# A hybrid decoder block: x's staging tiles moved into v's sum tiles, and the sums of the FFN's down weights moved from the first two dense products to the third and fourth

## The chip, the cores and the metric

The kernel runs on one core of one Trainium2 chip. The metric is the device time of one execution in microseconds (us); the time before the change is the median of three runs. A separate execution under the profiler gave the profile and the trace. Engines are named as in the profile: PE multiplies matrices (PEld loads its weights), DVE, ACT and POOL work on whole tiles, and SP issues nearly all DMA transfers, in one queue, in order.

## What is computed

One decoder block over 1024 tokens of width 1024: a Mamba-2 branch and a gated-linear-attention branch from one input projection, merged with sigmoid gates, then cross-attention to 256 memory tokens, then a SwiGLU feed-forward (FFN) and a last normalisation. Everything is float32. The parts that matter here:

```python
merged = sigmoid(g_ssd) * (y_ssd @ w_up_ssd) + sigmoid(g_gla) * (y_gla @ w_up_gla)
h = x + merged @ w_o                       # after the mixer
q = rmsnorm(h) @ w_xq                      # cross-attention's queries
k, v = split(rmsnorm(mem) @ w_xkv)         # its keys and values
...
h = h + (silu(g) * u) @ w_ffn_out          # D_FF = 2816 rows of w_ffn_out
```

## The kernel before, in words

Data lie transposed: a tile holds 128 features (or two or four times 128) by 512 or 1024 tokens, and `half(j)` is one of two halves of 512 tokens. Float32 products are made of three matmuls: every operand is split into a high and a low part (`split`: ACT writes the high part, DVE or POOL the difference), and high*high, low*high and high*low are summed in PSUM. Many of the large products go by a Strassen-like scheme of seven products of sums of blocks instead of eight (`CHAIN`: B11, B21, T1, B22, T2, T3, T4). Instructions are issued by a tile scheduler, which lists each engine's work in order of estimated time. Engines then run their own lists strictly in order and wait on semaphores. A tile that takes the place of another (same tag, or same slot of a pool) waits until the last reader of the older one is done, also when that reader is a DMA store. `slot("op")`, `slot("aux")` and `slot("m")` hand out large tiles from three pools; `vp` is a pool with tiles by name.

**The start (0 to about 100 us).** Three things run side by side. (1) `kv_unit`: the memory's keys and values, one 1 MB piece of `w_xkv` (`raw`) after another, stored to `vm_d` and `kT_d`. (2) `x_steps`: x is transposed on PE in 16 steps (two halves `j` of the tokens, 8 blocks `k` of features). Each step writes one PSUM bank; DVE makes the normalised block `hb` (profile name `hs`) from it, ACT copies the bank into a staging tile `xs` (L608), and every fourth step SP stores `xs` to `xT_d` (L610, 1 MB). The staging tile comes from `slot("op")`, the pool that also gives the operand tiles B11h, B21h, T1h and so on. (3) `v_steps`: GLA's v product by the chain of seven products; `vq` tiles hold its four output sums (`vq00` to `vq11`), `vsa` a sum of weights. The first product, B11, is copied to `vq10`, the second, B21, to `vq00`. SP's list also holds `late_constants`: two loads of `dcol` from `ssd_D` (L202), 1024 elements of four bytes each, and two small ones.

**The merge (848 to 1209 us).** Four dense products, called dense 0 to 3 here: y_ssd by w_up_ssd, y_gla by w_up_gla, merged by w_o, and the queries by w_xq. Each has 16 steps (8 blocks `o` of output features by two halves of tokens) of 24 matmuls of 128x128x512. Weights come as four `raw` pieces of 1 MB per product and are split into `wd` (two buffers) ahead of use by ACT, then DVE. After each step a `post` takes the PSUM bank (`acc`, four buffers). Dense 0's gates `gs_d` and dense 1's gates `gg_d` are loaded per block `o` into the tile `gates` (two halves, L1253): ACT applies the sigmoid (L1257), DVE multiplies, and dense 0 stores the product to `ysg_d` (L1262). Dense 1 loads it again by `ga` and adds it. Dense 2 adds x (`ga<-xT_d`), stores the sum to `h1_d` (in the order listings `h_d`), and sums squares into `ssum` on POOL, which PE adds up over features in dense 3 (`bank<-ones,ssum`).

**The sums of the down weights (`presum`).** For the FFN's last product the kernel forms four sums of blocks of `w_ffn_out` for each of 11 pieces `k`: load 1 MB into the tile `pre` (L1224), four additions of 128x512, four stores of 256 KB to `down_d` (L1228), and again with the same tile. `waiting(early, 5)` starts it five steps into dense 0; it is run with dense 0, 1, 2 and 3 at one step of `presum` per dense step, and in the trace it ran from 857 to 1029 us, beside dense 0 and 1. `either` picks POOL or DVE for each addition from the planner's costs; all 44 went to POOL.

Of the kernel before, what the change touches and what calls it, by code (L numbers as in the profile page):

```python
# [9 lines left out]
F32 = mybir.dt.float32  # L10
# [6 lines left out]
P = 128  # L17
TOK = 1024
D = 1024
# [59 lines left out]
def block_kernel(ctx: ExitStack, tc: tile.TileContext, t: dict, out: bass.AP):  # L79
# [196 lines left out]
    class Unit:  # L276
# [15 lines left out]
        def a(s, i, j):  # L292
            return s.raw[:, j * s.kh:(j + 1) * s.kh, i * P:(i + 1) * P]
# [145 lines left out]
    def run(main, *rest, prio=0):  # L439

        owed = [0.0] * len(rest)
        for _ in main:
            for i, (g, rate) in enumerate(rest):
                owed[i] += rate
                while owed[i] >= 1.0:
                    owed[i] -= 1.0
                    with tc.high_priority(offset=prio):
                        next(g, None)
# [101 lines left out]
    def kv_unit(c0):  # L550
# [32 lines left out]
        else:  # L583
            SP.dma_start(vm_d[:, c0 - D:c0 - D + 256].rearrange("(i p) c -> p i c", p=P), s)

    def x_steps():
        p = bank()
        spread(p, mss, 2)
        DVE.tensor_copy(mbc, p[:, :MEM])
        yield  # L590
        for j in range(2):
            for c in range(4 * j, 4 * j + 4):
                ACT.activation(msq, wide(xt[c // 2][:, c % 2]), AF.Square, accum_out=xr[:, c:c + 1])
            rsqrt(xr[:, 4 * j:4 * j + 4], xr[:, 4 * j:4 * j + 4], 1.0 / D)
            yield
            p = bank()
            spread(p, xr[:, 4 * j:4 * j + 4], 4)
            ACT.activation(rbc[:, half(j)], p, AF.Copy)
            yield
            for k in range(NB):  # L600
                if k % 4 == 0:
                    xs = slot("op", (P, 4, HALF), name="xs")
                p = bank()
                for a in range(4):
                    c = 4 * j + a
                    PE.transpose(p[:, a * P:(a + 1) * P], xt[c // 2][:, c % 2, k * P:(k + 1) * P], ident)
                DVE.scalar_tensor_tensor(hb[k][:, half(j)], p, col("norm_mix", k), rbc[:, half(j)], ALU.mult, ALU.mult)
                ACT.activation(xs[:, k % 4], p, AF.Copy)  # L608
                if k % 4 == 3:
                    SP.dma_start(xT_d[(k - 3) * P:(k + 1) * P, half(j)].rearrange("(k p) s -> p k s", p=P), xs)  # L610
                yield

    B = Operands(hb, 4)
# [4 lines left out]

    dt_t = cp.tile([P, NCH, NH], F32, name="dt_t")
    a1_t = cp.tile([P, NCH, NH], F32, name="a1_t")  # L620
    HW = 264

    vraw = {}

    def load_v(pr):
# [237 lines left out]
    class SSD:  # L863
# [62 lines left out]
        def gate(s):  # L926
            s.y = sp_.tile([P, 4, CH], F32, name="y", tag="y", bufs=3)
            for k in range(4):
                DVE.scalar_tensor_tensor(s.y[:, k], s.L[:, k], dcol[:, s.g * 4 + k:s.g * 4 + k + 1],
                                         s.py[:, k * P:(k + 1) * P], ALU.mult, ALU.add)  # L930
            mul(POOL, s.y, s.y, s.L[:, 4:8])
            sq = sp_.tile([P, 4, CH], F32, name="sq", tag="sq", bufs=1)
            ACT.activation(sq, s.y, AF.Square)
            s.rd = sp_.tile([P, CH], F32, name="rd", tag="rd", bufs=2)
            DVE.tensor_reduce(s.rd, sq.rearrange("p k s -> p s k"), AX.X, ALU.add)
# [239 lines left out]
    def dense(no, ins, post, pre=lambda o, j: None, js=JS):  # L1175

        todo = [(o, j) for o in range(NB) for j in (js if o + 1 < NB else js[::-1])]
        got = [pre(*x) for x in todo[:2]]
        for n, (o, j) in enumerate(todo):
            w = left[NB * no + o]  # L1180
            if n + 2 < len(todo):
                got.append(pre(*todo[n + 2]))
            cur = got[n]
            p = acc()
            m = 0
            for k in range(NB):
# [10 lines left out]
    def fetch(src, dst):  # L1197

        for k in range(NB):
            x = hl(dst, k)  # L1200
            raw = x[:, 1].bitcast(F32)
            SP.dma_start(raw, src[k * P:(k + 1) * P, :])
            ACT.activation(x[:, 0], raw, AF.Copy)
            sub(DVE, x[:, 1], raw, x[:, 0])
            yield
# [10 lines left out]
    sums["m"] = pool("sa2", 2, stack=st5)  # L1216
    s1 = Stats(rp)

    def presum():


        r = slot("m", (P, 2, D), name="pre")
        for k in range(KP):
            SP.dma_start(r, t["w_ffn_out"][256 * k:256 * k + 256, :].rearrange("(j p) c -> p j c", p=P))  # L1224
            yield
            a = lambda i, j: r[:, j, half(i)]
            s1_ = sums["m"].tile([P, HALF], F32, name="sa", tag="sa", bufs=2)
            put = lambda n, ap: SP.dma_start(down_d[(n * KP + k) * P:(n * KP + k + 1) * P, :], ap)  # L1228
            e = lambda: either(s1_, 1.0)
            add(e(), s1_, a(1, 0), a(1, 1))  # L1230
            put(0, s1_)
            yield
            sub(e(), a(1, 1), s1_, a(0, 0))
            put(1, a(1, 1))
            yield
            sub(e(), a(1, 0), a(0, 0), a(1, 0))
            put(2, a(1, 0))
            yield
            sub(e(), a(0, 1), a(0, 1), a(1, 1))
            put(3, a(0, 1))  # L1240
            yield

    def quad_of(src):
        return lambda o, j: quad(src, o * P, 0, j)

    gates = slot("m", (P, 2, TOK), name="gates")
    met = set()

    def gate(src, o, j):

        if (id(src), o) not in met:
            met.add((id(src), o))
            SP.dma_start(gates[:, o % 2], src[o * P:(o + 1) * P, :])  # L1253
        return gates[:, o % 2, half(j)]

    def gated(g, p):
        ACT.activation(g, g, AF.Sigmoid)  # L1257
# [23 lines left out]
        ACT.activation(h, q, AF.Copy, scale=g)  # L1281
        DVE.scalar_tensor_tensor(l, q, g, h, ALU.mult, ALU.subtract)

    def waiting(g, n):
        for _ in range(n):
            yield
        for _ in g:
            yield

    early = presum()  # L1290
    run(dense(0, i_ys, post_ys, lambda o, j: gate(gs_d, o, j)), (fetch(yg_d, i_yg), 0.5), (waiting(early, 5), 1.0))
    run(dense(1, i_yg, post_yg, lambda o, j: (gate(gg_d, o, j), quad(ysg_d, o * P, 0, j))), (early, 1.0))
    run(dense(2, i_wo, residual(h1_d, s1, "norm_xattn", put_xq), quad_of(xT_d)), (early, 1.0))


    kv = []
# [17 lines left out]
        DVE.tensor_scalar(xsc, s1.r, XSC, None, ALU.mult)  # L1314
        yield

    run(dense(3, i_xq, lambda o, j, p, g: into(i_q, o, j, p)), (xq_side(), 1.0), (early, 1.0))
    drain(early)
    load_kv(0)
    u_xo_stats = Stats(rp)  # L1320
# [331 lines left out]
```

## Time and profile before

| What | us |
|---|---|
| runs, median of 3 | 2020.72 (2018.88 to 2021.11) |
| the profiled execution's own time | 2022.57 |
| its span in the trace | 2020.5 |
| DVE, ACT, POOL busy | 1313.8, 860.8, 656.3 |
| mean granted PE clock | 0.992 |

The span is the time from the first to the last instruction in the trace. In the profile's rows a group reads "line engine operation output<-input", and a wait reads "who waits, for whom: us in total, times, longest". Windows give the busy time of each engine in a stretch, with the number of instructions in brackets. PEclk is the clock that PE was granted, as a share of full speed; the DMA share is the mean busy share of 16 DMA engines.

### The profile page before, as it was taken

Reading aid. Unit: us, or ns where it says so; the run is one execution under the profiler, and the core shown is the slowest. Engines: PE = TensorE matmul, PEld = TensorE weight load, DVE = VectorE, ACT = ScalarE, POOL = GpSimd, SP = SyncE. Lnnn points to the kernel's source line nnn. Section 1 sums busy time; section 2 is a strip of 40 time slices with the busy share of each in tenths; the row PEclk is TensorE's granted clock in tenths of the full one; section 3 lists DMA queues with packets and bytes.
Section 4 is the critical chain, followed back from the end, with each engine's and each line's share of the span. In section 5 each row is a group of like instructions: output and inputs, shape, how many; then the busy total and the mean of one; then the engine's idle time right before and its main releaser. Section 6 shows DMA issues by size and latency. Waiting matters only on the chain.

```text
span 2020.5 us, 26310 instructions
## 1 busy us (share of the span) xinstructions
PE 1953.7 (97%) x9772; PEld 1620.7 (80%) x9772; DVE 1313.8 (65%) x1869; ACT 860.8 (43%) x1482; POOL 656.3 (32%) x480
## 2 busy tenths in 40 slices
PE   7899899999999989999999999999999999999998
PEld 7899678877777777787788888877888888887887
DVE  6856679979886656532454227478777777774565
ACT  7434745465552455432233226453333333354243
POOL 4421243455653212023322100255444444430002
PEclk9899999999999999999999999999999999999999
DMA  7532233356553655797773210433224223276463
GB/s 247 194 117 88 94 124 116 113 181 190 168 173 110 208 163 177 244 357 244 289 237 132 80 42 22 139 124 108 79 89 134 90 82 114 77 259 218 152 227 129
DMA packets 241635, 309.58 MB, mean 153 GB/s; under 512 B 17354, under 2 KB 165044, under 8 KB 241508
## 3 DMA queue, kind: packets, MB, share of 16 engines
q1 hardware_dynamic: 241508, 307.91, 45.2%
q8 instruction: 77, 1.26, 0.3%
q14 instruction: 50, 0.41, 0.1%
HBM read 211.07 MB, written 96.80 MB: 152 GB/s over the span
## 4 chain that ended last, share of the span: by engine, by line
PE 46%; DVE 3%; DMA 2%; issue 1%; POOL 1%; ACT 1%; SPq 0%; POOLq 0%; ACTq 0%; DVEq 0%
PE acc L51 41%; PE bank L51 4%; DMA gates<-gg_d 1%; DMA fr<-act_d 1%; DVE fs L73 1%; PE bank L55 1%; POOL ssum L73 0%; POOL pre L73 0%; DMA pre<-in_w_ffn_out_dram 0%; DMA down_d<-pre 0%; DMA ysg_d<-gates 0%; DVE o L73 0%; DVE wlo L73 0%; DVE T2l L73 0%; DVE T4l L73 0%
## 5 line engine op out<-in xcount | busy, mean ns | idle before, releaser
L51 PE MATMUL acc<-hl,wd 128*128 128x512 f32 x1920 | 443.4, 391 | 6.0 <-DVE wd L73 2.9
L51 PEld LDWEIGHTS acc<-hl,wd 128*128 128x128 f32 x1920 | 360.4, 188 | 84.9 <-DVE wd L73 5.5
L73 DVE TENSOR_TENSOR wlo<-raw,whi 128x512 fp32r<-128x512 f32 x264 | 243.2, 925 | 77.1 <-ACT whi L223 76.8
L223 ACT ACTIVATE whi<-raw 128x512 fp32r<-128x512 f32 x272 | 170.2, 629 | 253.1 <-PE acc L51 224.8
L73 DVE TENSOR_TENSOR o<-acc,o 128x512 f32<-128x512 f32 (+1 forms) x256 | 172.5, 675 | 112.9 <-PE acc L51 100.6
L51 PE MATMUL acc<-fs 128*128 128x512 f32 (+1 forms) x792 | 156.0, 356 | 1.6 <-ACT o L1547 1.5
L51 PEld LDWEIGHTS acc<-fs 128*128 128x128 f32 x792 | 130.6, 189 | 22.7 <-ACT o L1547 1.9
L73 POOL TENSOR_TENSOR raw<-raw,sa 128x512 f32<-128x512 f32 x48 | 65.3, 1361 | 252.8 <-DVE wlo L73 247.1
L223 ACT ACTIVATE fs<-fr 128x1024 fp32r<-128x1024 f32 (+1 forms) x84 | 80.0, 984 | 112.7 <-PE acc L51 38.5
L73 DVE TENSOR_TENSOR fs<-fr,fs 128x1024 fp32r<-128x1024 f32 (+1 forms) x84 | 99.8, 1218 | 38.7 <-ACT fs L223 38.1
L73 DVE TENSOR_TENSOR wd<-raw,wd 128x1024 fp32r<-128x1024 f32 x40 | 50.3, 1260 | 83.1 <-ACT wd L223 82.9
L223 ACT ACTIVATE whi<-sa 128x512 fp32r<-128x512 f32 x96 | 60.0, 626 | 103.5 <-PE acc L51 103.4
L73 POOL TENSOR_TENSOR sa<-raw 128x512 f32<-128x512 f32 x47 | 74.0, 1575 | 86.2 <-DMA raw<-in_w_in_dram 47.7
L73 DVE TENSOR_TENSOR wlo<-sa,whi 128x512 fp32r<-128x512 f32 x96 | 82.6, 861 | 22.8 <-ACT whi L223 21.3
L73 POOL TENSOR_TENSOR raw<-raw 128x512 f32<-128x512 f32 x48 | 81.6, 1702 | 4.9 <-DVE sa L73 4.9
L73 POOL TENSOR_TENSOR ssum<-ssum,sq 128x512 f32<-128x512 f32 (+1 forms) x23 | 35.2, 1531 | 146.9 <-ACT sq L490 143.0
L51 PE MATMUL acc<-B21h,whi 128*128 128x512 f32 x192 | 76.9, 401 | 3.1 <-ACT o L353 3.1
L51 PE MATMUL acc<-T1h,whi 128*128 128x512 f32 x192 | 76.7, 399 | 2.7 <-ACT whi L223 2.7
L73 POOL TENSOR_TENSOR o<-o 128x512 f32<-128x512 f32 x29 | 49.2, 1703 | 91.1 <-DVE o L73 80.8
L51 PE MATMUL acc<-B21h,wlo 128*128 128x512 f32 x192 | 76.3, 398 | 2.5 <-DVE wlo L73 2.5
L51 PE MATMUL acc<-T1h,wlo 128*128 128x512 f32 x192 | 77.4, 403 | 0.5 <-DVE wlo L73 0.5
L51 PE MATMUL acc<-B22h,wlo 128*128 128x512 f32 x192 | 77.5, 404 | 0.0
(375 smaller groups left out, 4801.5 us busy)
## 6 DMA issues: line engine op xcount, KB each, us to landing
raw<-in_w_in_dram SPq DMA_DIRECT2D x26, 1024.0 KB, 5.7
raw<-in_w_ffn_in_dram SPq DMA_DIRECT2D x22, 1024.0 KB, 6.3
act_d<-o SPq DMA_DIRECT2D x77, 256.0 KB, 2.1
fr<-act_d SPq DMA_DIRECT2D x35, 512.0 KB, 6.8
pre<-in_w_ffn_out_dram SPq DMA_DIRECT2D x11, 1024.0 KB, 8.6
fr<-down_d SPq DMA_DIRECT2D x20, 512.0 KB, 3.7
down_d<-pre SPq DMA_DIRECT2D x33, 256.0 KB, 3.4
raw<-in_w_xkv_dram SPq DMA_DIRECT2D x8, 1024.0 KB, 11.4
```

The lines of the kernel that those rows point to most:

```text
L51: return s.e.matmul(o, x, y, **kw)
L55: return s.e.transpose(o, x, i)
L73: return f(*a, **kw)
L223: ACT.activation(hi, src, AF.Copy)
```

## The change

No arithmetic is added or left out. Two things are moved.

The first: `x_steps` no longer takes four staging tiles of four blocks from the "op" pool, but eight tiles of two blocks in `vp`, under the tags of v's sums (`XS_HOME`). So there are eight stores of 512 KB instead of four of 1 MB; from the sixth staging tile on, a tile takes the place of an older staging tile, and v's `vq` and `vsa` tiles take the place of staging tiles.

The second: the two "m" slots, before one for `gates` and one for `pre`, become `pair`. Beside dense 0 and 1 they hold four blocks of gates, which are loaded as far as two blocks ahead of the one that is asked for; beside dense 2 and 3 they hold two pieces of `w_ffn_out`, the piece after next being loaded as soon as the fourth store of a piece has landed.

```diff
+    XS_HOME = ("vq10", "vq00", "vq11", "vq01", "vsa", "vq00", "vq11", "vq01")
...
-                if k % 4 == 0:
-                    xs = slot("op", (P, 4, HALF), name="xs")
+                if k % 2 == 0:
+                    xs = vp.tile([P, 4, HW], F32, name="xs", tag=XS_HOME[4 * j + k // 2])
+                    xs = xs.rearrange("p a b -> p (a b)")[:, :2 * HALF].rearrange("p (k s) -> p k s", k=2)
...
-                ACT.activation(xs[:, k % 4], p, AF.Copy)
-                if k % 4 == 3:
-                    SP.dma_start(xT_d[(k - 3) * P:(k + 1) * P, half(j)].rearrange("(k p) s -> p k s", p=P), xs)
+                ACT.activation(xs[:, k % 2], p, AF.Copy)
+                if k % 2:
+                    SP.dma_start(xT_d[(k - 1) * P:(k + 1) * P, half(j)].rearrange("(k p) s -> p k s", p=P), xs)
...
+    pair = [slot("m", (P, 2, TOK), name="pair") for _ in range(2)]
     def presum():
-        r = slot("m", (P, 2, D), name="pre")
+        def load(k):
+            if k < KP:
+                SP.dma_start(pair[k % 2], t["w_ffn_out"][256 * k:256 * k + 256, :].rearrange("(j p) c -> p j c", p=P))
+        load(0)
+        load(1)
         for k in range(KP):
-            SP.dma_start(r, t["w_ffn_out"][256 * k:256 * k + 256, :].rearrange("(j p) c -> p j c", p=P))
-            yield
-            a = lambda i, j: r[:, j, half(i)]
+            a = lambda i, j: pair[k % 2][:, j, half(i)]
...
             put(3, a(0, 1))
+            load(k + 2)
             yield
...
-    gates = slot("m", (P, 2, TOK), name="gates")
-    met = set()
+    gate_seq, gate_got = [(s, o) for s in (gs_d, gg_d) for o in range(NB)], [0]
     def gate(src, o, j):
-        if (id(src), o) not in met:
-            met.add((id(src), o))
-            SP.dma_start(gates[:, o % 2], src[o * P:(o + 1) * P, :])
-        return gates[:, o % 2, half(j)]
+        n = gate_seq.index((src, o))
+        while gate_got[0] < min(n + 3, len(gate_seq)):
+            m = gate_got[0]
+            s_, o_ = gate_seq[m]
+            SP.dma_start(pair[m % 4 // 2][:, m % 2], s_[o_ * P:(o_ + 1) * P, :])
+            gate_got[0] += 1
+        return pair[n % 4 // 2][:, n % 2, half(j)]
...
-    run(dense(0, i_ys, post_ys, lambda o, j: gate(gs_d, o, j)), (fetch(yg_d, i_yg), 0.5), (waiting(early, 5), 1.0))
-    run(dense(1, i_yg, post_yg, lambda o, j: (gate(gg_d, o, j), quad(ysg_d, o * P, 0, j))), (early, 1.0))
-    run(dense(2, i_wo, residual(h1_d, s1, "norm_xattn", put_xq), quad_of(xT_d)), (early, 1.0))
+    run(dense(0, i_ys, post_ys, lambda o, j: gate(gs_d, o, j)), (fetch(yg_d, i_yg), 0.5))
+    run(dense(1, i_yg, post_yg, lambda o, j: (gate(gg_d, o, j), quad(ysg_d, o * P, 0, j))))
+    early = presum()
+    run(dense(2, i_wo, residual(h1_d, s1, "norm_xattn", put_xq), quad_of(xT_d)), (early, 1.1))
...
-    run(dense(3, i_xq, lambda o, j, p, g: into(i_q, o, j, p)), (xq_side(), 1.0), (early, 1.0))
+    run(dense(3, i_xq, lambda o, j, p, g: into(i_q, o, j, p)), (xq_side(), 1.0), (early, 1.75))
```

The scheduler then lists the work in another order. Three places of these lists follow.

ACT at the start, where x's second half is staged. Before:

```order
L223 ACTIVATE B11h<-hs 128x512 x4
L608 ACTIVATE xs<-bank 128x512 x4
L223 ACTIVATE B21h<-hs 128x512 x4
L608 ACTIVATE xs<-bank 128x512
L223 ACTIVATE T1h<-hs 128x512 x2
L608 ACTIVATE xs<-bank 128x512
L684 ACTIVATE vq<-acc 128x264
L223 ACTIVATE T1h<-hs 128x512
L684 ACTIVATE vq<-acc 128x264
```

The same place in the change:

```order
L223 ACTIVATE T1h<-hs 128x512 x2
L687 ACTIVATE vq<-acc 128x264 x4
L223 ACTIVATE T1h<-hs 128x512
L613 ACTIVATE xs<-bank 128x512 x2
L223 ACTIVATE T1h<-hs 128x512
L223 ACTIVATE B22h<-hs 128x512 x3
L613 ACTIVATE xs<-bank 128x512 x2
L223 ACTIVATE B22h<-hs 128x512
L613 ACTIVATE xs<-bank 128x512 x2
L223 ACTIVATE whi<-raw 128x512
L223 ACTIVATE whi<-vraw 128x528 x2
```

Before, T1h took the "op" slot of the first staging tile and so waited for its store. Now `vq` (`vq10`) waits for the first store and the three `xs x2` groups for the second, third and fourth; the splits of kv's and v's weights stand behind all of them.

SP at the start, before:

```order
L513 DMA raw<-in_w_xkv_dram 128x8x256
L202 DMA dcol<-in_ssd_D_dram 64x8x1 x2
L204 DMA dtb<-in_ssd_dt_bias_dram 128x16
L205 DMA alog<-in_ssd_A_log_dram 128x16
L584 DMA vm_d<-kvs 128x2x256 x2
L513 DMA raw<-in_w_xkv_dram 128x8x256
L610 DMA xT_d<-xs 128x4x512
L584 DMA vm_d<-kvs 128x2x256
```

And in the change:

```order
L513 DMA raw<-in_w_xkv_dram 128x8x256 x2
L202 DMA dcol<-in_ssd_D_dram 64x8x1 x2
L204 DMA dtb<-in_ssd_dt_bias_dram 128x16
L205 DMA alog<-in_ssd_A_log_dram 128x16
L584 DMA vm_d<-kvs 128x2x256 x2
L513 DMA raw<-in_w_xkv_dram 128x8x256
L615 DMA xT_d<-xs 128x2x512 x2
L513 DMA raw<-in_w_xkv_dram 128x8x256
L615 DMA xT_d<-xs 128x2x512
L584 DMA vm_d<-kvs 128x2x256
```

One more piece of w_xkv is issued ahead of the two `dcol` loads, and the smaller stores follow them among the next pieces.

SP and DVE in the merge. In dense 1 SP's list before mixed gates and `presum`:

```order
L1224 DMA pre<-in_w_ffn_out_dram 128x2x1024
L1123 DMA ga<-ysg_d 128x512
L1253 DMA gates<-gg_d 128x1024
L1228 DMA down_d<-sa 128x512
L1123 DMA ga<-ysg_d 128x512
L1228 DMA down_d<-pre 128x512 x3
L1224 DMA pre<-in_w_ffn_out_dram 128x2x1024
```

In the change `presum` stands in dense 2's part of SP's list, with two loads and eight stores to about three steps:

```order
L1229 DMA pair<-in_w_ffn_out_dram 128x2x1024
L1126 DMA ga<-xT_d 128x512
L1284 DMA h_d<-ga 128x512
L1229 DMA pair<-in_w_ffn_out_dram 128x2x1024
L1284 DMA h_d<-ga 128x512
L1236 DMA down_d<-sa 128x512
L1306 DMA ga<-kT_d 128x2x256
L1236 DMA down_d<-pair 128x512 x3
```

DVE at the end of dense 2 in the change, where `ga<-acc,ga` is the last of its 16 additions of x:

```order
L73 SCALAR_TENSOR_TENSOR hl<-ga,cols,hl 128x512
L73 TENSOR_TENSOR pair<-sa,pair 128x512
L73 TENSOR_TENSOR sa<-pair 128x512
L73 TENSOR_TENSOR ga<-acc,ga 128x512
L73 TENSOR_TENSOR pair<-pair 128x512
L73 TENSOR_TENSOR wd<-raw,wd 128x1024
```

Here `sa<-pair` is the first addition of the eleventh piece: DVE, which before had none of `presum`'s additions, has 12 of the 44 now, and the last addition of x stands behind one that needs the last load of `w_ffn_out`.

More of the change, by code (lines that the diff above doesn't have):

```diff
@@ L584, in kv_unit @@
             SP.dma_start(vm_d[:, c0 - D:c0 - D + 256].rearrange("(i p) c -> p i c", p=P), s)
+    HW = 264
+    XS_HOME = ("vq10", "vq00", "vq11", "vq01", "vsa", "vq00", "vq11", "vq01")
     def x_steps():
@@ L620, in block_kernel @@
     a1_t = cp.tile([P, NCH, NH], F32, name="a1_t")
-    HW = 264
     vraw = {}
@@ L1282, in put_xq @@
         DVE.scalar_tensor_tensor(l, q, g, h, ALU.mult, ALU.subtract)
[L1284 to L1288, printed above, removed]
+    run(dense(0, i_ys, post_ys, lambda o, j: gate(gs_d, o, j)), (fetch(yg_d, i_yg), 0.5))
+    run(dense(1, i_yg, post_yg, lambda o, j: (gate(gg_d, o, j), quad(ysg_d, o * P, 0, j))))
     early = presum()
-    run(dense(0, i_ys, post_ys, lambda o, j: gate(gs_d, o, j)), (fetch(yg_d, i_yg), 0.5), (waiting(early, 5), 1.0))
-    run(dense(1, i_yg, post_yg, lambda o, j: (gate(gg_d, o, j), quad(ysg_d, o * P, 0, j))), (early, 1.0))
-    run(dense(2, i_wo, residual(h1_d, s1, "norm_xattn", put_xq), quad_of(xT_d)), (early, 1.0))
+    run(dense(2, i_wo, residual(h1_d, s1, "norm_xattn", put_xq), quad_of(xT_d)), (early, 1.1))
     kv = []
```

## The prediction

> **What bounds the kernel now.** I read the page first, for how busy each engine is.
>
> ```profile
> span 2020.5 us, 26310 instructions
> PE 1953.7 (97%) x9772; PEld 1620.7 (80%) x9772; DVE 1313.8 (65%) x1869; ACT 860.8 (43%) x1482; POOL 656.3 (32%) x480
> ```
>
> PE is busy for all but 67 us of the span. No matmul is added or removed, so time can only be won where PE stands or runs at a low clock, and lost where it is newly made to stand. Next come windows cut at the borders of the four dense products, each 384 matmuls long, and at the start.
>
> ```profile
> core 0: us, PE busy (x) PEld busy (x) DVE busy (x) ACT busy (x) POOL busy (x), PEclk, DMA share, GB/s
> 848.04:937.20 89.16, 87.82 (x385) 71.84 (x384) 31.63 (x35) 25.31 (x32) 23.26 (x16) 1.00 0.87 304
> 937.20:1032.94 95.74, 91.08 (x385) 72.60 (x384) 43.44 (x53) 24.88 (x38) 39.13 (x28) 0.98 0.78 280
> 1032.94:1119.99 87.05, 87.05 (x385) 72.07 (x384) 38.66 (x49) 29.97 (x45) 19.76 (x13) 1.00 0.48 157
> 36.00:72.00 36.00, 23.99 (x134) 21.93 (x135) 30.62 (x31) 18.11 (x37) 27.40 (x16) 0.72 0.77 266
> 72.00:108.00 36.00, 35.84 (x298) 35.55 (x297) 27.30 (x41) 17.97 (x35) 7.53 (x6) 1.00 0.17 57
> ```
>
> Dense 2 does its 384 matmuls in 87.05 us without a gap: that is the floor. Dense 1 needs 95.74 for the same, so 8.69 us are lost there. The start loses more: 134 matmuls in 36 us against 298 in the next 36, partly at a clock of 0.72.
>
> Why dense 1 loses is read from who waits for the gates, from the chain there (start, us, what), and from what presum transfers beside it (KB each, median us from issue to landing).
>
> ```profile
>   DMA gates<-gg_d: 53.1, 8
>   DMA gates<-gs_d: 27.9, 6
>   ACT gates L1257: 81.0, 14
> 945.84 2.73 DMA down_d<-pre
> 948.59 0.38 SPq L1224
> 949.03 5.52 DMA ysg_d<-gates
> 954.60 4.21 DMA gates<-gg_d
> 960.04 0.96 ACT wd L223
> 961.03 0.55 DVE wd L73
> 976.58 8.06 DMA gates<-gg_d
> 985.87 0.96 ACT wd L223
> 986.85 1.24 DVE wd L73
> 988.13 11.89 PE acc L51 x44
> pre<-in_w_ffn_out_dram SPq DMA_DIRECT2D x6, 1024.0 KB, 7.3
> down_d<-pre SPq DMA_DIRECT2D x21, 256.0 KB, 3.4
> ```
>
> With two halves, a block of gates can be loaded only once the block two before it is stored to ysg_d or used; that store stands in SP's queue behind presum's stores and load; the load then takes 4 to 8 us beside presum's traffic; ACT waits for it 53.1 us in dense 1, and the split of the next weights (`wd`) stands behind it on ACT. PE waits for wd.
>
> **Part one: the gates.** In the change the gates lie four halves deep and are asked for one block (10.9 us, two steps of 5.44) earlier, and presum is gone from this part of SP's queue. The longest load above, 8.06 us, fits in that block. Dense 1 then has its old traffic of 280 GB/s * 95.74 us = 26.8 MB less six loads of 1.05 MB and 28 stores of 0.26 MB (21 from `pre`, and a third as many from `sa`), about 13 MB, as little as dense 2 carried without a gap. The floor says that no more than **8.7 us** can come from here; the least is 0. I take -8.7, and give back 0.4 for weights that are late for other reasons. Dense 0's 2.1 us over the floor fall at its first weights, before any gate is used: nothing.
>
> **Part two: presum beside dense 2.** What it costs there is the dear question. These are its rows before, the rates that DMA has reached, and the last work of dense 2's sums.
>
> ```profile
> L73 DVE TENSOR_TENSOR gates<-gates,ga x16: 691/692/1070, 950.8 to 1036.7; 128x512 f32<-128x512 f32 x16
> L73 POOL TENSOR_TENSOR pre<-pre x22: 1286/1293/2282, 870.7 to 1027.6; 128x512 f32<-128x512 f32 x22
> DMA to landing us min/median/max: 3.1/4.3/9.8
> SPq L1224 <- DMA down_d<-pre: 15.8, 11, 3.4
> 870.00:890.00 20.00, 20.00 (x90) 16.57 (x89) 9.94 (x10) 6.57 (x8) 4.18 (x3) 1.00 1.05 381
> 950.00:970.00 20.00, 19.19 (x82) 15.21 (x83) 6.51 (x10) 4.57 (x8) 8.22 (x7) 1.00 0.85 314
> 1122.24 1.85 POOL L73 TENSOR_TENSOR ssum<-ssum,sq 128x512 f32<-128x512 f32 x1 [4.11 <-ACT sq L490]
> 1136.31 0.28 PE L51 MATMUL bank<-ones,ssum 128*128 128x1 f32 x2
> ```
>
> In SP's list nine of the eleven loads and 37 of the 44 stores stand between dense 2's first and last step: 9 * 1.05 + 37 * 0.26 = 19.1 MB. Dense 2 carried 157 GB/s * 87.05 us = 13.7 MB. Together 32.8 MB in 87.05 us, or 377 GB/s: as much as the best stretch above (381) and more than the stretch where presum paced itself (314). So DMA will be full, and at the rates between these two the list ends 1 us early to 17.4 us late.
>
> How late may it be? The last load's additions stand ahead of dense 2's last `ssum` on POOL and of its last addition of x on DVE. Before, the last ssum ended at 1124.1 and PE read it at 1136.3: 12.2 us of slack, of which three additions (one on DVE at 0.69 us, two on POOL at 1.29) take 3.3. About 9 us are left. Dense 2's own input has more: SP's list asks for x about five steps, 27 us, ahead. The engines have the time: 32 additions of 1.29 us and 16 sums of at most 1.85 make 71 of POOL's 87 us; DVE's 12 additions add 8 us to 38.7.
>
> So dense 2 loses nothing down to 32.8 MB / 96 us = 342 GB/s, and 8.5 us at 314. The lists wait for only one landing per load (15.8 us over eleven loads before), and now have another piece under way meanwhile; I take a rate near 350 and **+0.5 us** (bounds 0 and +8.5, and past that only if the rate falls below what was seen with one tile).
>
> **Part three: the start.** The rows of the wait that goes, of what SP issued, and of the splits behind it:
>
> ```profile
> ACT T1h L223 <- DMA xT_d<-xs: 7.6, 1, 7.6
> 34.10 2.86 SPq L202 DMA_DIRECT2D dcol<-in_ssd_D_dram  x2
> 43.02 4.93 SPq L610 DMA_DIRECT2D xT_d<-xs  x1
> 40.00:44.00 4.00, 1.27 (x8) 0.96 (x8) 3.76 (x5) 3.52 (x7) 2.53 (x2) 0.96 0.05 0
> 44.00:48.00 4.00, 3.53 (x16) 3.53 (x17) 4.00 (x5) 3.78 (x8) 2.88 (x2) 0.50 0.10 21
> 56.00:60.00 4.00, 0.82 (x4) 0.82 (x5) 0.78 (x2) 2.50 (x6) 1.73 (x2) 0.67 1.07 397
> 57.49 1.15 ACT L223 ACTIVATE T1h<-hs 128x512 fp32r<-128x512 f32 x2 [7.59 <-DMA xT_d<-xs]
> 60.83 0.66 ACT L223 ACTIVATE whi<-raw 128x512 fp32r<-128x512 f32 x1
> 67.91 0.64 ACT L223 ACTIVATE whi<-vraw 128x528 fp32r<-128x528 f32 x1 [4.58 <-PE bank L51]
> ```
>
> From 40 to 47.5 us almost nothing moved: the two dcol loads, 1024 elements of four bytes, hold the queue. Only then did the first store get through, and T1h, which had its slot, waited to 57.49. The change removes that wait and puts four on ACT: `vq` for the first store and three pairs of `xs` for the next three. When do these land? One more 1 MB piece goes ahead of dcol, at 397 GB/s 2.6 us, so the empty stretch ends at about 50. Behind it stand two vm_d stores, a piece and the first store, 0.5 + 1.05 + 0.5 MB: 5.3 us and some 2.5 to the landing, 58. The second lands 1.3 us later, the third after another piece, 63.5, the fourth at about 65.5. The splits of kv's weights (60.83 before) are listed behind all four and begin near 66; those of v's (67.91), which set when the next chain product begins, near 68 to 69. In return B11's product and the operands T1h and B22h are made earlier. I take **+1.5 us**. Bounds: -4, if the earlier work fills PE's gaps; +7, if everything behind the first wait moves by the 5 to 7 us of the kv splits.
>
> A rule of the Trainium skill speaks against these stores: its page "DMA: Bandwidth & Descriptors" (Rules for kernel authors) asks for at least 1 MiB per DMA, and its section on the anatomy of one DMA fits 2.0 us plus bytes over 436e3, which is 3.2 us for each of eight stores against 4.4 for each of four. One after another that would be 8 us more, an estimate from that page, and the sum would end at about +2. The trace agrees only in part: the fastest 1 MB load above landed in 3.1 us, below that fit.
>
> **The sum.** -8.7 + 0.4 + 0.5 + 1.5 = -6.3 us, on the profiled execution: span 2020.5 to 2014.2, its own time 2022.57 to 2016.3. The median of the runs lies 1.85 us below the profiled execution, so I predict 2020.72 - 6.3 = **2014.4 us**.
>
> **Rivals.** (1) *Presum paces dense 2.* If loads and stores of two pieces run in step, DMA empties whenever SP waits for a landing. Dense 1 ran at 280 GB/s for such reasons; at 300, 32.8 MB take 109.3 us, 22.3 late less 9 of slack, +13.3 and in all +6.5: 2027. The kernel is slower than before once the list is more than 15.8 us late, below 319 GB/s. Against it: the second tile. (2) *ACT's four waits cost their full price*, +7 at the start: -1 in all, 2019.9. For it: ACT runs in order, and kv's splits stand behind the last wait; against it: the next product hangs on v's splits, which PE let wait till 67.91 anyway. (3) *The start gains*: PE gets B11's matmuls into the stretch that was empty and the stores land before ACT comes to them, so that the 7.6 us go: -15.4 in all, 2005.3. Beside this, the Trainium skill's page "TensorE: Matmul & The Clock Gate" (Part 1) says that the clock halves after about 3.4 us of idling; the rows above agree (0.50 from 44 to 48 us, after a window with 1.27 us of matmuls), so shorter gaps would also keep the clock. (4) *The gates stay late*, because other transfers held them up: dense 1 keeps its 8.7 us and the rest adds 2: 2022.7.
>
> **How the numbers follow.** Forecast 0.53, rivals (1) 0.17, (2) 0.16, (3) 0.08, (4) 0.06. The forecast's own range is 2010 to 2019, from the bounds of its terms. To hold 8 in 10 the range takes in most of (2) and the near part of (1) and of (3): 2007 to 2025. About 0.2%, 4 us, is what a measurement of this kernel tells from no change: faster means below 2016.7, slower above 2024.8. Faster: four fifths of the forecast and all of (3), 0.50. Slower: most of (1) and a little of (2) and (4), 0.18. The rest, 0.32, is no change.
>
> **What would show it.** Right: dense 1 in 87 to 88 us, ACT's wait for `pair<-gg_d` near zero; dense 2 in under 88.5 us at 350 GB/s or more; PE's first `bank<-ones,ssum` without a wait; at the start T1h without a wait, and waits of ACT's `vq` and `xs` for `xT_d<-xs` that end at 58 to 66 us. Wrong: PE idle at the end of dense 2 behind DVE's `sa<-pair` or POOL's `ssum`, or the next chain product later than 77 us or earlier than 69.

## The result, and the profile after

The changed kernel is slower: a median of 2024.97 us in 21 runs (2020.07 to 2029.54) against 2020.72 us in 21 runs of the kernel before (2016.14 to 2027.86), a ratio of 1.0020 (95% interval 1.0012 to 1.0027). That is about 4 us more, where 6 us less were forecast. The profiled execution took 2022.31 us, with a span of 2020.6. It lies 2.7 us under its own median, and the one before lay 1.85 us over its median, so the two traces, with spans of 2020.5 and 2020.6, show where single stages differ, but not the 4 us.

The windows of the changed kernel, cut at the same borders as before: dense 1, dense 2, dense 3 with the wait at its start, and the start of the kernel.

```profile
core 0: us, PE busy (x) PEld busy (x) DVE busy (x) ACT busy (x) POOL busy (x), PEclk, DMA share, GB/s
937.83:1024.87 87.04, 87.04 (x386) 72.10 (x384) 43.45 (x54) 23.34 (x33) 6.85 (x4) 1.00 0.43 149
1024.87:1111.92 87.05, 86.92 (x384) 71.67 (x383) 50.22 (x48) 26.09 (x37) 52.28 (x35) 1.00 0.92 323
1111.92:1208.64 96.72, 91.67 (x405) 75.26 (x404) 31.42 (x38) 21.53 (x32) 13.93 (x10) 0.98 0.34 117
36.00:72.00 36.00, 20.11 (x141) 18.77 (x141) 22.25 (x33) 19.54 (x39) 20.39 (x15) 0.76 0.80 278
72.00:108.00 36.00, 33.15 (x271) 32.47 (x270) 27.09 (x33) 13.83 (x26) 12.09 (x7) 1.00 0.12 41
```

Dense 1 now runs at its floor, 87.04 us instead of 95.74: the expected 8.7 us are there. Dense 2 and 3 together take 1208.64 - 1024.87 = 183.77 us; before, they took 1209.06 - 1032.95 = 176.11, so 7.7 us went back at the border between them. Of these PE stood for 183.77 - 178.58 = 5.2; in the other 2.5 it was busy longer with the same 787 matmuls, at a granted clock of 0.98 behind the border where it was 1.00 before. And from 36 to 108 us PE did 412 matmuls where it had done 432.

What happened at the border is in the timelines of DVE and ACT before, and of SP, DVE, ACT and PE in the change (start, us, engine, line, operation, count, and in brackets the idle time before it with its releaser). The first two rows are the kernel before.

```profile
1120.19 0.69 DVE L73 TENSOR_TENSOR ga<-acc,ga 128x512 f32<-128x512 f32 x1 [3.21 <-PE acc L51]
...
1120.93 0.71 ACT L1281 ACTIVATE hl<-ga,cols 128x512 fp32r<-128x512 f32 x1
...
1112.03 0.37 SPq L1229 DMA_DIRECT2D pair<-in_w_ffn_out_dram  x1
...
1117.31 1.76 DVE L73 TENSOR_TENSOR pair<-sa,pair 128x512 f32<-128x512 f32 x1 [3.00 <-POOL sa L73]
1121.00 0.96 DVE L73 TENSOR_TENSOR sa<-pair 128x512 f32<-128x512 f32 x1 [1.93 <-DMA pair<-in_w_ffn_out_dram]
1121.88 0.68 DVE L73 TENSOR_TENSOR ga<-acc,ga 128x512 f32<-128x512 f32 x1
...
1122.59 0.72 ACT L1292 ACTIVATE hl<-ga,cols 128x512 fp32r<-128x512 f32 x1 [7.60 <-DVE ga L73]
...
1123.37 3.69 PE L51 MATMUL acc<-hl,wd 128*128 128x512 f32 x8 [4.30 <-ACT hl L1292]
```

Before, the last addition of x in dense 2 waited for PE alone. In the change the last load of w_ffn_out was issued at 1112.0. Its first addition, `sa<-pair`, waited for it on DVE until 1121.0. The last addition of x (`ga<-acc`) stood behind that one, ACT's split behind the addition, and PE behind the split.

At the start ACT's timeline shows the wait that the change brought, and PE's row what it did to PE.

```profile
58.02 1.24 ACT L687 ACTIVATE vq<-acc 128x264 f32<-128x264 f32 x4 [9.84 <-DMA xT_d<-xs]
59.64 1.11 ACT L613 ACTIVATE xs<-bank 128x512 f32<-128x512 f32 x2
63.89 1.06 ACT L613 ACTIVATE xs<-bank 128x512 f32<-128x512 f32 x2
65.59 1.09 ACT L613 ACTIVATE xs<-bank 128x512 f32<-128x512 f32 x2
69.80 0.64 ACT L223 ACTIVATE whi<-raw 128x512 fp32r<-128x512 f32 x1 [3.13 <-PE bank L51]
70.56 1.37 ACT L223 ACTIVATE whi<-vraw 128x528 fp32r<-128x528 f32 x2
...
60.31 1.97 PE L55 MATMUL bank<-ident,xt 128*128 128x128 f32 x8 [12.71 <-ACT xs L613]
```

`vq` waited 9.84 us for the first store, and PE stood for 12.71 us, since all four `bank` tiles held transposes of x that ACT had not copied yet. The other `xs` rows show no wait for a store.

### The profile page after: what moved, and what is told of

It reads as the page before. It is cut to its first block, busy times and chain, and to the rows that moved or that the text cites. A ratio compares the mean times of both kernels' runs of the same rounds, so it can differ in the third digit from the quotient of the medians.

```text
span 2020.6 us, 26344 instructions
## 1 busy us (share of the span) xinstructions
PE 1951.7 (97%) x9772; PEld 1621.2 (80%) x9772; DVE 1329.8 (66%) x1881; ACT 863.4 (43%) x1482; POOL 640.9 (32%) x468
## 4 chain that ended last, share of the span: by engine, by line
PE 50%; DMA 4%; DVE 3%; POOL 2%; issue 1%; ACT 1%; SPq 0%; POOLq 0%; DVEq 0%; ACTq 0%
PE acc L51 45%; PE bank L51 5%; POOL pair L73 1%; PE bank L55 1%; DMA pair<-in_w_ffn_out_dram 1%; DMA down_d<-pair 1%; DMA fr<-act_d 1%; DVE fs L73 1%; POOL ssum L73 1%; DMA h_d<-ga 0%; POOL sa L73 0%; DVE hl L73 0%; DMA hl<-ys_d 0%; DVE o L73 0%; DMA ga<-xT_d 0%
## 5 line engine op out<-in xcount | busy, mean ns | idle before, releaser
L73 POOL TENSOR_TENSOR sa<-pair 128x512 f32<-128x512 f32 x9 | 12.0, 1341 | 208.2 <-DMA pair<-in_w_ffn_out_dram 181.7
```

The costliest lines, as they stand in the source:

```text
L73: return f(*a, **kw)
```

## The experiments

Each run was timed beside the kernel before on the same chip; the ratio is to that. "Merge" stands for the changed kernel with x staged as before. The last two columns are lengths in the run's own trace: dense 1 (floor 87.04), and dense 2 and 3 together (176.11 before).

| Run | median us | before | ratio (95% interval) | dense 1 | dense 2 and 3 |
|---|---|---|---|---|---|
| changed (from the section above) | 2024.97 | 2020.72 | 1.0020 (1.0012 to 1.0027) | 87.04 | 183.77 |
| x alone | 2031.76 | 2023.22 | 1.0044 (1.0029 to 1.0058) | 100.70 | 177.05 |
| merge alone | 2021.79 | 2023.22 | 1.0000 (0.9990 to 1.0011) | 87.04 | 187.42 |
| before, ssd_D as a row | 2020.89 | 2023.22 | 0.9994 (0.9985 to 1.0004) | 97.94 | 177.06 |
| changed, ssd_D as a row | 2021.53 | 2023.22 | 0.9994 (0.9985 to 1.0002) | 87.04 | 184.74 |
| changed, nine pieces | 2022.97 | 2022.02 | 1.0005 (0.9992 to 1.0017) | 87.04 | 181.78 |
| changed, additions on POOL | 2025.06 | 2022.02 | 1.0021 (1.0008 to 1.0034) | 87.04 | 186.16 |
| changed, one tile | 2033.55 | 2022.02 | 1.0059 (1.0041 to 1.0077) | 87.04 | 193.07 |
| merge, one tile, ssd_D as a row | 2023.69 | 2022.02 | 1.0008 (0.9994 to 1.0022) | 87.04 | 192.10 |
| changed, ssum on DVE | 2023.77 | 2022.85 | 1.0006 (0.9997 to 1.0014) | 87.04 | 183.38 |
| changed, held back | 2016.58 | 2022.85 | 0.9964 (0.9952 to 0.9976) | 87.04 | 176.11 |
| merge, held back, ssd_D as a row | 2010.17 | 2022.85 | 0.9936 (0.9923 to 0.9948) | 87.04 | 176.11 |
| merge, ssum on DVE, ssd_D as a row | 2016.48 | 2022.85 | 0.9960 (0.9947 to 0.9973) | 87.04 | 183.26 |

### The two parts, each alone

The kernel before with the new staging of x only:

```diff
-                    xs = slot("op", (P, 4, HALF), name="xs")
+                    xs = vp.tile([P, 4, HW], F32, name="xs", tag=XS_HOME[4 * j + k // 2])
...
```

> Only the staging of x is changed, the merge is as before. Theory A (the start costs what the profiles show, where PE is 3.8 us later at the 400th matmul and still 3.1 later at the 880th): +3 to +4.5 us against before, with ACT's vq waiting 8 to 10 us for the first store of x and PE without a matmul for 10 us or more between 46 and 62 us. Theory B (those microseconds are absorbed or made good before dense 0, where PE was only 0.7 us later): within 1.5 us of before.

The waits of PE and ACT from 20 to 110 us in that run, and its dense 1:

```profile
PE bank L55 <- ACT xs L613: 16.8, 4, 14.1
ACT vq L687 <- DMA xT_d<-xs: 11.1, 1, 11.1
...
941.50:1042.20 100.70, 90.91 (x385) 72.46 (x383) 39.59 (x51) 24.41 (x38) 38.24 (x28) 0.97 0.75 268
```

The time is 8.9 us longer (5.9 to 11.7), more than either theory said. The start shows theory A's waits, and dense 0 begins 4.0 us later than before in this trace. Most of the rest is in dense 1, 5.0 us longer than before, though the edit does not touch it: the scheduler lists `presum`'s stores and loads in dense 0 and 1 in another order here, and the gates are loaded as tightly as before. Whether the order or chance costs the 5.0 us is not shown; 97.94 us in another kernel with the old gates says that dense 1 varies.

The changed kernel with x staged as before, that is the kernel before with the gates and `presum` of the change (the edit is against the changed kernel):

```diff
-                    xs = vp.tile([P, 4, HW], F32, name="xs", tag=XS_HOME[4 * j + k // 2])
...
+                    xs = slot("op", (P, 4, HALF), name="xs")
...
```

> Only the gates and the sums of the down weights are changed, the start is as before. Theory A (dense 1 gives 8.5 us, and the sums, late at the end of dense 2, take 7 to 8 of them back at the border to dense 3): -2 to 0 us against before, dense 1 at 87.1 us, a wait of PE for ACT's hl of 3 to 5 us near 1118 us. Theory B (the whole of the 4 us comes from the merge): +3 to +5 us.

Its windows, dense 1 and then dense 2 with 3; the third row is the kernel before, dense 2 with 3:

```profile
934.81:1021.85 87.04, 87.04 (x385) 72.07 (x384) 43.63 (x54) 22.95 (x33) 6.85 (x4) 1.00 0.44 149
1021.85:1209.27 187.42, 180.49 (x787) 148.30 (x786) 81.56 (x85) 47.60 (x69) 66.21 (x44) 0.97 0.60 210
...
1032.95:1209.06 176.11, 176.11 (x787) 146.10 (x786) 60.03 (x77) 47.92 (x70) 23.63 (x16) 1.00 0.32 105
```

Theory A: the part wins 8.7 us in dense 1 and loses 11.3 in dense 2 and 3, and the time is the same as before (1.0000). So the 0.2% of the whole change come from the start, by subtraction. The traces bear that out. PE's 880th matmul begins at 141.0 us in both traces with the old staging and the old load of ssd_D, and at 143.1 to 145.2 in the seven with the new staging; dense 0 begins at 845.4 and 848.0 there, and at 848.7 to 852.8 here. In its own trace dense 0 of the changed kernel begins the earliest of these seven, which hides the loss in its span.

### What holds up the stores of x

`ssd_D` is loaded as one row of 16 values into each partition and spread by two copies on DVE, in the kernel before and in the changed one:

```diff
+        SP.dma_start(drow, t["ssd_D"].partition_broadcast(P))
         for a in range(2):
-            SP.dma_start(dcol[a * 64:(a + 1) * 64, :],
-                          t["ssd_D"].rearrange("(j a) -> a j", a=2)[a].partition_broadcast(64))
+            DVE.tensor_copy(dcol[a * 64:(a + 1) * 64, :],
+                            drow[a * 64:(a + 1) * 64, :].rearrange("p (j a) -> p a j", a=2)[:, a])
```

> The kernel before, with ssd_D loaded as one row of 64 bytes per partition and spread to dcol by two copies on DVE, instead of two loads of 512 elements of four bytes. Theory A (those loads empty the queue from 40 to 47.5 us and so hold the first store of x): no stretch without traffic there, T1h's wait of 7.6 us for the store gone or under 2 us, and 4 to 10 us faster. Theory B (the store is late because 1 MB pieces of weights stand ahead of it): T1h still waits 5 us or more, within 2 us of before.

> The changed kernel with the same other load of ssd_D. Theory A: the first store of x lands 7 to 9 us earlier, ACT's vq waits under 3 us for it instead of 9.8, and the kernel is 6 to 11 us faster than the changed one, that is 2 to 7 us faster than before. Theory B (the stores wait for each other and for the pieces): vq's wait stays above 6 us and the time within 2 us of the changed kernel.

A window of the changed kernel without the row, one of the kernel before with the row, two of the changed kernel with the row, and there the only wait of ACT that was left for a store of x:

```profile
44.00:48.00 4.00, 3.33 (x28) 2.86 (x26) 3.99 (x7) 2.68 (x5) 2.99 (x3) 1.00 0.05 2
...
44.00:48.00 4.00, 3.21 (x14) 2.91 (x15) 3.94 (x8) 3.97 (x9) 0.89 (x1) 0.50 1.08 393
...
40.00:44.00 4.00, 4.00 (x36) 4.00 (x36) 2.01 (x5) 2.64 (x5) 0.00 (x0) 1.00 0.85 262
44.00:48.00 4.00, 1.81 (x15) 1.34 (x13) 3.96 (x8) 1.79 (x4) 1.75 (x2) 1.00 1.08 386
...
ACT vq L689 <- DMA xT_d<-xs: 0.6, 1, 0.6
```

From 44 to 48 us DMA moves 393 and 386 GB/s; without the row it was 21 in the kernel before and 2 in the changed one. Theory A's mechanism holds: `vq`'s wait of 9.8 us is 0.6. Its sizes do not hold for the kernel before: T1h's wait is gone and the time barely moves (0.9994, interval across 1). In its trace dense 0 begins at 841.7 us instead of 848.0, but dense 0 and 1, with the old gates, take 190.5 us instead of 184.9 and give most of that back; one trace of each does not tell how much of it is chance. In the changed kernel the ratio falls from 1.0020 to 0.9994, about 5 us, a little less than the 6 to 11 of theory A. Whether the new staging still costs something with the row is open, since the merge part with the row and nothing else was not run. In the traces with the row PE's 880th matmul begins at 141.2 us with the new staging (one trace) and at 138.7 to 140.7 with the old (four).

### What holds up the border

The changed kernel without the loads and sums of the last two pieces of `presum`, so that the last eight stores write other data:

```diff
-            if k < KP:
+            if k < KP - 2:
...
-        for k in range(KP):
+        for k in range(KP - 2):
...
+        for k in range(KP - 2, KP):
+            for n in range(4):
+                SP.dma_start(down_d[(n * KP + k) * P:(n * KP + k + 1) * P, :], pair[0][:, n // 2, half(n % 2)])
+                yield
```

> The changed kernel without the loads and additions of the last two of the eleven pieces of w_ffn_out; their eight stores write tiles that are there. Theory A (PE's wait near 1118 us is presum's list being late: the last piece's addition stands ahead of the last addition of x on DVE): that wait is gone, dense 3's first 96 matmuls take 24 us instead of 31, and the kernel is 6 to 9 us faster than the changed one, 2 to 5 faster than before. Theory B (PE waits there because DMA as a whole is too slow for x and the weights in dense 2): the wait stays at 3 us or more.

The first 87.05 us from the beginning of its dense 2 (the length without a loss; the same in the rows of the runs below), then dense 2 with 3, and PE's wait for hl:

```profile
1030.65:1117.70 87.05, 85.76 (x378) 70.69 (x377) 48.97 (x47) 25.72 (x37) 52.09 (x34) 1.00 0.92 326
1030.65:1212.43 181.78, 178.36 (x787) 147.10 (x786) 77.05 (x82) 47.61 (x69) 58.33 (x39) 0.99 0.59 205
...
PE acc L51 <- ACT hl L1296: 2.1, 1, 2.1
```

Of 7.7 us 5.7 stay, and PE's wait for ACT's hl is 2.1 us instead of 4.3. The ratio falls from 1.0020 to 1.0005, about 3 us, where theory A had 6 to 9. That is between the theories: it is not the last piece alone.

The changed kernel with all additions on POOL:

```diff
-            e = lambda: either(s1_, 1.0)
+            e = lambda: POOL
```

> The changed kernel with all 44 additions on POOL. Theory A (it is the place in DVE's queue that hurts): PE no longer waits for ACT's hl at the border, POOL is then 90 per cent busy in dense 2 and ends its sums later, so that a part comes back as a wait of PE at bank<-ones,ssum; 2 to 6 us faster than the changed kernel. Theory C (the cost is the sums being late as such, wherever they stand): PE waits 5 us or more at bank<-ones,ssum or for weights behind ACT's sq, and the time is within 2 us of the changed kernel or longer.

Its ACT timeline at the border, and PE's wait for hl:

```profile
1114.43 0.63 ACT L490 ACTIVATE sq<-ga 128x512 f32<-128x512 f32 x1 [6.77 <-POOL ssum L73]
...
1125.07 0.63 ACT L490 ACTIVATE sq<-ga 128x512 f32<-128x512 f32 x1 [5.55 <-POOL ssum L73]
1125.60 1.04 ACT L223 ACTIVATE wd<-raw 128x1024 fp32r<-128x1024 f32 x1
1126.55 0.71 ACT L1292 ACTIVATE hl<-ga,cols 128x512 fp32r<-128x512 f32 x1
...
PE acc L51 <- ACT hl L1292: 4.0, 1, 4.0
```

DVE is free of `presum`, and PE still waits 4.0 us for ACT's hl. The time is theory C's (1.0021 against 1.0020) and so is the way behind ACT's `sq`, though PE waits for hl and not for `ssum`. Dense 2's sum of squares stands on POOL behind additions that wait for loads (16.6 us in five waits from 1025 to 1180 us), `sq` on ACT waits for it (its tile has one buffer), and the weights and hl stand behind `sq`.

The changed kernel with one tile for the pieces, and the same on the merge part alone with ssd_D as a row:

```diff
-                SP.dma_start(pair[k % 2], t["w_ffn_out"][256 * k:256 * k + 256, :].rearrange("(j p) c -> p j c", p=P))
+                SP.dma_start(pair[0], t["w_ffn_out"][256 * k:256 * k + 256, :].rearrange("(j p) c -> p j c", p=P))
...
-        load(1)
...
-            a = lambda i, j: pair[k % 2][:, j, half(i)]
+            a = lambda i, j: pair[0][:, j, half(i)]
...
-            load(k + 2)
+            load(k + 1)
```

> The changed kernel with one tile for the pieces of w_ffn_out as before the change, beside dense 2 and 3. Theory A (two pieces under way fill DMA, which then falls behind the order of the lists): DMA moves under 310 GB/s in dense 2 and keeps up, PE's wait at the border is under 1 us, 6 to 9 us faster than the changed kernel. Theory B (in-order engines then wait for every load): DVE and POOL wait for each load, PE waits for wd or hl in dense 2, no gain over the changed kernel.

> x staged as before the change, gates four halves deep, one tile for the pieces of w_ffn_out beside dense 2 and 3, and ssd_D loaded as one row. Theory A: dense 1's 8.5 us, no loss at the border, and about 1.5 us at the start: 8 to 11 us faster than before. Theory B: the border still costs 5 us or more: 2 to 4 us faster than before.

The first 87.05 us of dense 2, and dense 2 with 3, of the first of them, and a place in DVE's queue:

```profile
1026.58:1113.63 87.05, 85.08 (x373) 69.60 (x372) 37.11 (x39) 23.20 (x33) 36.67 (x26) 1.00 0.75 258
1026.58:1219.65 193.07, 181.41 (x787) 148.19 (x786) 76.46 (x85) 47.41 (x69) 62.88 (x44) 0.97 0.60 204
...
1128.32 0.69 DVE L73 TENSOR_TENSOR sa<-pair 128x512 f32<-128x512 f32 x1 [4.67 <-DMA pair<-in_w_ffn_out_dram]
1129.05 0.69 DVE L73 TENSOR_TENSOR pair<-pair 128x512 f32<-128x512 f32 x1
1129.65 0.68 DVE L73 TENSOR_TENSOR ga<-acc,ga 128x512 f32<-128x512 f32 x1
```

This fells my theory that DMA is full: it moved 258 GB/s instead of 323, and dense 2 and 3 lost 17.0 us instead of 7.7. Theory B holds. What costs is that an in-order queue stands at an addition whose load has not landed; here DVE stands 4.67 us for one, with an addition of x two places behind it. The second of the two lost 16.0 us in dense 2 and 3 and ended at the time of before (1.0008), worse than its theory B, which had it 2 to 4 us faster.

So the next kernel leaves the traffic and clears the queues: all additions on POOL, and dense 2's sums of squares on DVE, on the changed kernel and on the merge part with ssd_D as a row:

```diff
-            e = lambda: either(s1_, 1.0)
+            e = lambda: POOL
...
-    s1 = Stats(rp)
+    s1 = Stats(rp, e=DVE)
```

> The changed kernel with all of presum's additions on POOL and dense 2's sums of squares (ssum) on DVE, so that no queue that PE waits for holds an addition that waits for a load of w_ffn_out. The traffic stays. Theory A (the loss at the border is the in-order queues of DVE, POOL and ACT, held up by additions that wait for loads): DMA at 300 GB/s or more as before, PE's wait for ACT's hl at the border under 1 us, 5 to 9 us faster than the changed kernel. Theory B (what is late is dense 2's own x, because DMA is full): DVE's ga waits for ga<-xT_d and PE's wait stays at 3 us or more.

In the next text "the run before" is the merge part with `presum` held back, which comes last in this section.

> The same as the run before, but with presum not held back: all its additions on POOL and dense 2's sums of squares on DVE. Theory A (the queues): 7 to 10 us faster than before. Theory B (DMA): 0 to 3 us faster than before, with PE's wait at the border.

The first one's dense 2, then ACT, DVE and PE's longest wait in dense 3:

```profile
1028.81:1115.86 87.05, 87.05 (x386) 72.08 (x385) 56.88 (x54) 27.09 (x40) 44.48 (x29) 1.00 0.86 298
...
1139.72 1.15 ACT L223 ACTIVATE kvhl<-ga 128x512 fp32r<-128x512 f32 x2 [21.70 <-DMA down_d<-pair]
...
1140.38 3.36 DVE L73 TENSOR_TENSOR kvhl<-ga,kvhl 128x512 fp32r<-128x512 f32 x2 [17.92 <-ACT kvhl L223]
1143.67 0.68 DVE L73 TENSOR_TENSOR hl<-acc,hl 128x512 fp32r<-128x512 f32 x1
...
PE acc L51 <- DVE hl L73: 4.9, 1, 4.9
```

The border is free, as theory A says: PE is busy all through dense 2. DMA moves 298 GB/s in that stretch, so traffic of that size does not stop PE by itself. But the loss moves on by some 20 us. `kvhl`, the split of attention's keys, takes a tile of `presum`, and the list has it early in dense 3; ACT stands 21.7 us for the last store from that tile, DVE behind ACT, and PE waits 4.9 us. Dense 2 and 3 again lose 7.3 us, and the kernel is about 3 us faster than the changed one, not 5 to 9. The second of the two is 0.40% faster than before, 8 us, the size of its theory A; but its trace loses 7.15 us in dense 2 and 3, so the theory's reason did not bring that size, and its trace, 3.5 us shorter than before, does not account for it.

Last, four pieces beside dense 2 and seven held back until its last sum (`last`), by a copy of one element that the loads must wait for. The seven are added on POOL, and `presum` is paced at 1.0 beside dense 2 instead of 1.1; which of these is needed was not separated:

```diff
         for k in range(KP):
+            if k == 4:
+                for i in range(2):
+                    POOL.tensor_copy(pair[i][0:1, 0, 0:1], last[0][0:1, 0:1])
+                load(4)
+                load(4 + 1)
...
-            e = lambda: either(s1_, 1.0)
+            e = lambda: POOL if k >= 4 else either(s1_, 1.0)
...
-            load(k + 2)
+            if k + 2 not in (4, 4 + 1):
+                load(k + 2)
...
+            last[0] = q
...
-    run(dense(2, i_wo, residual(h1_d, s1, "norm_xattn", put_xq), quad_of(xT_d)), (early, 1.1))
+    run(dense(2, i_wo, residual(h1_d, s1, "norm_xattn", put_xq), quad_of(xT_d)), (early, 1.0))
```

> The changed kernel with the first four pieces of w_ffn_out beside dense 2 and the other seven held back until the last addition of x in dense 2, by a one-element copy of that sum into the tiles, and these seven added on POOL. Theory A: nothing waits at the border, dense 3 in 89 to 90 us, 7 to 9 us faster than the changed kernel. Theory B (the loss moves on): PE waits as long in dense 3 for wd, or at the start of attention for kvhl.

> x staged as before the change, ssd_D loaded as one row, gates four halves deep, presum held back in the same way. Theory A: 8.5 us from dense 1, about 1.5 from the start, nothing lost at the border: 8 to 11 us faster than before. Theory B: as for the run before, 1 to 3 us faster than before.

Dense 2, and dense 2 with 3, of the second of them, and DVE's last addition of x in dense 2:

```profile
1021.35:1108.40 87.05, 87.05 (x386) 72.11 (x385) 38.19 (x41) 27.19 (x40) 35.78 (x25) 1.00 0.64 217
1021.35:1197.46 176.11, 176.11 (x787) 146.15 (x786) 63.42 (x73) 47.06 (x69) 79.19 (x58) 1.00 0.65 224
...
1108.59 0.69 DVE L73 TENSOR_TENSOR ga<-acc,ga 128x512 f32<-128x512 f32 x1 [3.21 <-PE acc L51]
```

Theory A's mechanism on both: dense 2 and 3 take 176.11 us, as before, with all of `presum` inside, and DVE's last addition waits for PE and for nothing else, as it did before the change. The gains are larger than theory A had them. The changed kernel becomes 0.36% faster than before instead of 0.20% slower, about 11 us where 7 to 9 were expected. With x staged as before and ssd_D as a row the kernel is 0.64% faster than before (0.52 to 0.77), 12.7 us where 8 to 11 were expected: the fastest of all that ran. Its trace is 11.3 us shorter than that of before: 8.7 in dense 1, and the beginning of dense 1 is 2.9 earlier.

## Why the prediction was wrong, point by point

**What bounds it, and part one, were right.** PE's standing was what could be won, dense 1's floor was 87.05 and it runs in 87.04. The 0.4 us that I gave back there were not needed. ACT's waits for `pair<-gg_d` in dense 1 are not near zero, as I had it: five are left, 15.1 us in all, but they reach no wait of PE.

**Part two failed**, at the step "I take a rate near 350 and +0.5 us" and at the "About 9 us are left" that it rests on. The rate was 323 GB/s, below the 342 that the step itself gave as the border of no loss. By its own formula 32.8 MB / 323 GB/s is 101.5 us, 14.5 late, less 9 of slack 5.5; the trace says 7.7, and 11.3 in the run with the merge part alone. The slack was read at the wrong place. I read it at the last `ssum`, which kept it: in the changed kernel it ends at 1127.2, and PE reads it at 1135.9. PE waited at the other place that I had named and not sized, behind DVE's last addition of x. Before, ACT's split of that sum ended at 1121.6, and the matmul that waits for it in the change, the 30th of dense 3, began at 1126.6: 4.9 us of slack, of which the same three additions leave 1.6. With that the formula gives 12.9, above the 7.7 and the 11.3, so it is no exact rule. And the reason behind the step fell as well: with 258 GB/s and slack in DMA the loss more than doubled. I had counted one slack, at one place, for the last load. In fact every queue that holds an addition or a tile of `presum` (DVE, POOL by `ssum` and `sq`, ACT by `kvhl`) can hand a late load on to PE, and clearing one of them sent the loss to the next.

**Part three had the direction and the landings, and a size too small.** Stores forecast to land at 58, 59.3, 63.5 and 65.5 us landed at 58.0, 59.3, 63.4 and 65.5, by the events of their semaphores in the trace. Only the first of the four waits on ACT came, the 9.84 us of `vq`; when ACT came to the three pairs of `xs`, their tiles were free to within 0.1 us. The splits behind them came at 69.8 and 70.6 instead of "near 66" and "near 68 to 69", because PE, which had stood for 12.7 us, now had transposes and kv's matmuls in front of the bank that the split needed. That these things made +1.5 into about +4 is argued from this one trace; the size itself is 1.0020 for the whole change against 1.0000 for the merge part, to the width of the intervals, and the 2 to 4 us in the traces at the 880th matmul.

**The rivals.** (1) named the right place and the right sign, and the wrong reason, as above: it had the kernel slower below 319 GB/s, and it was slower at 323. Of (2)'s four waits the first came; the start cost about 4 us, not 7. (3) and (4) did not come. The rule of the Trainium skill's page "DMA: Bandwidth & Descriptors" (Rules for kernel authors), at least 1 MiB per DMA, would have made eight stores of 512 KB cost 8 us by that page's fit, which the page gives for transfers issued on the GpSimd path, while these are issued from SP. The traces do not bear the 8 us out: with ssd_D as a row PE's 880th matmul begins at 141.2 us with the eight stores and at 138.7 to 140.7 with the four. The prediction's "fastest 1 MB load above landed in 3.1 us" was a misreading: that row holds the 256 KB stores from `pre` too, and 3.1 us is one of these. The fastest 1 MB load whose landing the trace before shows took 5.2 us, above the fit's 4.4.

**Together**: -8.7 for the gates, about +8 for `presum`, about +4 for the start, which is +3.3 where the runs say about +4. The forecast had -8.3, +0.5, +1.5. The traces leave open how much the old gates cost in an average run: dense 1 took 95.7, 97.9 and 100.7 us in three kernels that load them in the old way.

## What to carry to other kernels

Before background work is put beside a stage that is free of waits, ask of every in-order queue which of the stage's instructions will stand behind one that waits for a load, and of every tile who takes it next: slack at one of these places says nothing of the others. If a greedy order brings such work in early, tie it to the stage's last result instead of tuning its rate. A transfer that looks slow may be held by a small one ahead of it: look first for a stretch with no bytes moving.

## What the runs showed of the hardware that was not expected

Float32 additions of two tiles in SBUF do not run on DVE and POOL at the same time: the one that starts second waits for the other. These are three pairs of overlapping rows of the changed kernel, DVE's above POOL's:

```profile
1105.68 0.69 DVE L73 TENSOR_TENSOR pair<-sa,pair 128x512 f32<-128x512 f32 x1 [1.84 <-POOL sa L73]
1105.72 1.80 POOL L73 TENSOR_TENSOR pair<-pair 128x512 f32<-128x512 f32 x1
...
1107.99 1.77 DVE L73 TENSOR_TENSOR pair<-pair 128x512 f32<-128x512 f32 x1
1107.48 1.73 POOL L73 TENSOR_TENSOR ssum<-ssum,sq 128x512 f32<-128x512 f32 x1
...
1103.16 0.68 DVE L73 TENSOR_TENSOR ga<-acc,ga 128x512 f32<-128x512 f32 x1
1102.65 1.74 POOL L73 TENSOR_TENSOR pair<-pair 128x512 f32<-128x512 f32 x1
```

In the first pair DVE starts 0.04 us ahead and takes its usual 0.69 us, and POOL takes 1.80 instead of 1.29. In the second POOL starts ahead, and DVE takes 1.77. In the third DVE reads one of its inputs from PSUM and takes 0.68 us beside a busy POOL. With POOL idle DVE's addition of two SBUF tiles took 0.69 us at 1128.32 in the run with one tile. The prediction had costed three additions at 3.3 us with 0.69 for DVE's. The Trainium skill's page "GPSIMD Engine Reference" (Specifications) says that POOL shares its SBUF interfaces with VectorE, with contention for DVE instructions with two SBUF inputs; the trace agrees, and gives the size, a factor of 2.6 for DVE's addition and 1.4 for POOL's.

Two loads of 512 elements of four bytes each, 4 KB in all, left DMA at 0 to 21 GB/s from 40 to 48 us in the kernel before, with megabytes issued behind them. With ssd_D as one load of 64 bytes per partition there is no such stretch in the changed kernel, and 2.4 us under 60 GB/s are left of it in the kernel before (40.0 to 42.4 us).
